# Modulation blocks 24 to 39 of a hybrid decoder layer, given other places in the order of the work

## The chip, the cores and the metric

The kernel runs on one core of a Trainium2 chip. The metric is the device time of one execution in microseconds (us). The kernel before was timed three times: 430.69, 431.64 and 430.80 us, median 430.8 us. The engines are TensorE (PE for the matmuls, PEld for their weight loads), VectorE (DVE), ScalarE (ACT), GpSimd (POOL) and SyncE (SP, which issues nearly all DMAs here).

## The reference

One layer of a decoder, 256 positions, width 1024, all in float32. A vector `c` conditions it, through a matrix of 6144 x 1024:

```python
mod = silu(c) @ w_ada + b_ada             # 6144 numbers: shift1 scale1 gate1 shift2 scale2 gate2
h = rms_norm(x, norm1_g) * (1 + scale1) + shift1
x = x + gate1 * mixer(h)                  # in-projection; attention and SSD; out-projection w_out
h = rms_norm(x, norm2_g) * (1 + scale2) + shift2
x = x + gate2 * conv_ffn(h)               # w_up, convolution over 3 positions, SwiGLU, w_down
```

The mixer projects `h` to q, k, v (8 heads of 128), z, x/B/C and dt. One half is causal softmax attention with normalized q and k. The other is a state-space part (SSD): convolution and SiLU on x/B/C, then for each of 16 heads a 256 x 256 causal matrix of decays times C·B, times x·dt, plus a skip term, times SiLU(z), normalized. Both halves, side by side, go through `w_out`.

## The kernel before, in words

Everything is transposed: channels on the 128 partitions, positions along the rows. Weights come as chunks of 128 x 1024 floats (512 KB), one DMA each on SP's queue (L146), into a ring of eight buffers `raw`. Nearly every chunk is split for a product of higher precision: ACT rounds it to `whi` (L189), DVE takes the rest into `wlo` (L191), and PE does three matmuls where one would stand (`mm3`, L344: whi·hhi, wlo·hhi, whi·hlo). A few chunks (`PLAIN`) go to PE unsplit, in plain float32 (L826).

The 6144 modulation numbers are 48 blocks of 128. A block is a tile `ada` of 128 x 1024 (512 KB, L152) from a ring of three buffers, and one DVE instruction multiplies it with silu(c) and sums along the row (`ada_dve`, L244 to L248). Blocks 0 to 15 (shift1, scale1) are needed at once and are done first. Blocks 16 to 23 are gate1, 24 to 31 scale2, 32 to 39 shift2; blocks 40 to 47 (gate2) go to POOL and ACT in the FFN. The eight gate1 values get their bias at unit 28 (L787); scale2 is used when the last stage before the FFN begins (L867), shift2 after that (L880).

The order is written as units of one weight chunk each. Unit 0 to 4 is the rest of z, 5 to 28 is q, k and v (four chunks for each half of q, of k and of v), 29 to 36 the part of the out-projection that reads the SSD, 37 to 44 the part that reads the attention. Side work is hung on units by the table `P` (L45): `put(u, f)` files a function under unit u and `side(u)` (L789) runs what is filed. `P['ada_u']` holds the 24 units at which blocks 16 to 39 are multiplied (L780 to L786). It is sorted before use (L118). The load of a block enters SP's queue behind the chunk that lies four units later (`ada_lead`, L119 to L125), or when the ring has a free buffer.

Outside the stretches marked by hand, PE, DVE, ACT and POOL are ordered by the framework's scheduler: it takes the program as recorded, plans times for it, and writes a fixed order for each engine. SP keeps the order in which the DMAs were recorded (L70). So another place for a block moves its own DMA and its own DVE instruction by hand, and what stands around them on every engine through the planner.

The steps that the prediction speaks of: `ab_load` (L573, one DMA of a row of sums, broadcast to 128 partitions, out of `acd`), `decay` (L580: ACT L584, L585 and L590, DVE L591), `ssd_y` (L595: PE L602 and L603, then DVE L604 and L606), `qk_evac` (L642: ACT L644 and L648), `qk_rsqrt` (L654), `k_scale` (L659: ACT L662), `qk_trans` (L664: PE L668), `scores` (L681: PE L683 and L684, DVE L689 to L692, ACT L694), `ptrans` (L707: PE L711), `pv` (L716: PE L719 and L720, DVE L724), `ssm_out` (L633, by `scaled` at L627: DVE L629, ACT L630, DVE L631), `attn_sum` (L727: PE L611).

Of the kernel before, what the change touches and what calls it, by code (L numbers as in the profile page):

```python
# [41 lines left out]
V_DTB = 326  # L42
V_ALL = 327

P = {'n2l': 6, 'sqa': 0, 'xr0': 0, 'scp': 1, 'vq': 1, 'v1': 6, 'n2': 4, 'hpx': [1, 0, 1, 0, 0, 1], 'e0': 0, 'ev': [1, 0, 1, 0], 'ada_u': [3, 4, 5, 5, 6, 7, 10, 9, 9, 19, 20, 20, 22, 24, 24, 25, 33, 35, 36, 37, 39, 39, 41, 42], 'ada_e': [1, 1, 1, 1, 1, 1, 1, 1, 1, 1, 1, 1, 1, 1, 1, 1, 1, 1, 1, 1, 1, 1, 1, 1], 'ada_lead': 4, 'ada_s': 0, 'g2': 68, 'hip': [0, 0, 0, 0, 0, 0, 0, 0, 0, 0, 0, 0, 0, 0, 0, 0, 0, 0, 0, 0, 0, 0, 0, 0, 0, 0, 0, 0, 0, 0, 1, 0, 0, 0, 1, 0, 0, 0, 0, 1, 0, 0, 0, 0, 0, 0, 0, 0, 0, 0, 0, 0, 0, 0, 0, 0, 0, 0, 0, 0], 'conv': [0, 0, 1, 0, 2, 5, 5, 4, 8, 4, 7, 6], 'dt': [1, 2, 2, 4], 'cdb': [7, 7], 'xbt': [9, 12, 11, 12], 'Y0': 14, 'DL': 3, 'ab0': 11, 'ss': 9, 'so': 2, 'qk': [12, 14, 17, 20, 21, 23], 'A0': 21, 'so1': 2, 'so2': 3, 'pv0': 26, 'sm_e': [0, 0, 1, 0, 1, 0, 0, 0], 'dc_e': [2, 2, 2, 0, 2, 2, 2, 0, 2, 2, 2, 0, 2, 2, 2, 0], 'mm_e': [1, 1, 1, 1, 1, 1, 1, 1, 1, 1, 1, 1, 1, 1, 1, 1], 'gz_e': [0, 0, 0, 0, 0, 0, 0, 0], 'sq_e': [1, 1, 1, 1, 1, 1, 1, 1], 'final': 2, 'ab_q': 0, 'LA': 2, 'asu': 34, 'aru': 38, 'aod': 2, 'w0': 4, 'w1': 4, 'w2': 4, 's1la': -1, 'zi': 1, 'lop': [0, 0, 0, 0, 0, 0, 0, 0, 0, 0, 0, 0, 0, 0, 0, 0, 0, 0, 0, 0, 0, 0, 0, 0, 0, 0, 0, 0, 0, 0, 0, 0, 0, 0, 0, 0, 0, 0, 0, 0, 0, 0, 0, 0, 0, 0, 0, 0, 0, 0, 0, 0, 0, 0, 0, 0, 0, 0, 0, 0], 'subs': [2, 1, 1, 1, 1, 1, 1, 1, 1, 1, 1, 1, 1, 1, 1, 1], 's1a': [0, 1, 0, 1, 0, 0, 0, 0]}  # L45

@with_exitstack
def mixer_ffn(ctx: ExitStack, tc: tile.TileContext, xT_d, c_d, vec_d, alog_d, ada_d,
# [24 lines left out]

    RAW, HL, ADA, LA = 8, 5, 3, P["LA"]
    raw_r = Ring(RAW, [128, 1024], "raw")
# [6 lines left out]
    for kt in range(KT):  # L82
        chunks.append((win1_d[kt, :, 0:1024], 1024))
        cuts.append(P["subs"][kt])
        if kt == 0:
            chunks.append((wv0_d, 1024))
            cuts.append(2)
        chunks.append((win1_d[kt, :, 1024:1936], 912))
        cuts.append(P["subs"][KT + kt])
    N1 = len(chunks)  # L90
# [11 lines left out]
    NCHUNK = len(chunks)  # L102
    items = [("a", 0), ("v", 0), ("a", 1)] if P["vq"] else [("a", 0), ("a", 1), ("v", 0)]
    for kt in range(KT):
        items.append(("w", 2 * kt + (kt > 0)))
        if kt == 0 and P["e0"] == 0:
            items.append(("w", 1))
        if kt < KT - 1:
            items.append(("a", 2 * kt + 2))
            if P["s1a"][kt]:  # L110
                items.append(("a", 2 * kt + 3))
# [953 lines left out]
```

## Time and profile before

| | |
|---|---|
| median of three runs | 430.8 us |
| profiled execution, its own time | 430.68 us |
| span of that execution | 429.0 us |
| PE busy, PEld busy | 422.5 us, 385.1 us |
| DVE busy, ACT busy, POOL busy | 344.4 us, 268.2 us, 26.0 us |
| DMA, mean over the span | 224 GB/s |

The span runs from the first to the last instruction of the profile; the time of the execution is 1.7 us longer. A busy share is an average over stages: up to about 60 us the first projection runs beside the first 16 modulation blocks, up to 84 us z, up to about 175 us q, k and v with the SSD and the first attention heads beside them, up to 233 us the out-projection, then the FFN. Instruction ends of PE are modelled and overlap the next start, so that a regular row of starts, and not the busy time, shows that PE is fed.

### The profile page before, as it was taken

To read this page: it belongs to the slowest core of one execution; us is meant where nothing else is said; L and a number is where in the kernel's file an instruction comes from. 1 tells how busy PE (TensorE), PEld (TensorE's weight loads), DVE (VectorE), ACT (ScalarE), POOL (GpSimd) and SP (SyncE) were. 2 spreads that over 40 slices of the span, in tenths; PEclk is the share of its full clock that TensorE was granted. 3 is DMA by queue.
4 is the path that set the end of the run, shared out by engine and by line. 5 is a ranking of instruction groups with operands and counts; after the bars stand their busy time and mean duration, and the time that the engine had idled before them with its cause. 6 is when DMAs were issued, how large, how long until landed. Compare 5 with 4: busy or idle time off the path is not lost.

```text
span 429.0 us, 7921 instructions
## 1 busy us (share of the span) xinstructions
PE 422.5 (98%) x3020; PEld 385.1 (90%) x3020; DVE 344.4 (80%) x680; ACT 268.2 (63%) x534; POOL 26.0 (6%) x24
## 2 busy tenths in 40 slices
PE   8999999999999999999999999999999999999996
PEld 8899998768767567889999999999999999999996
DVE  4779968999659888999999699778787877777755
ACT  4375448826999775886267495576666655555640
POOL 2000000000000001000000000222332200000000
PEclk9899999999999999999999999999999999999999
DMA  7999965889359549234691468767776665554002
GB/s 270 398 414 408 388 195 179 306 313 339 103 178 384 185 150 377 100 136 165 232 348 55 136 249 278 270 219 257 261 244 207 236 197 198 161 185 148 0 2 98
DMA packets 29589, 96.19 MB, mean 224 GB/s; under 512 B 3680, under 2 KB 6128, under 8 KB 29552
## 3 DMA queue, kind: packets, MB, share of 16 engines
q1 hardware_dynamic: 29520, 95.68, 62.5%
q8 instruction: 23, 0.38, 0.4%
q14 instruction: 14, 0.11, 0.1%
q10 hardware_dynamic: 32, 0.02, 0.0%
HBM read 94.62 MB, written 1.06 MB: 223 GB/s over the span
## 4 chain that ended last, share of the span: by engine, by line
PE 78%; DVE 9%; DMA 6%; ACT 5%; issue 1%; SPq 1%; ACTq 0%
PE bank L347 17%; PE bank L345 17%; PE bank L346 17%; PE bank L826 4%; PE bank L805 4%; PE bank L828 4%; DMA raw<-in_win_dram 4%; PE bank L829 4%; PE bank L830 4%; DVE wlo L191 2%; DMA vec<-in_vec_dram 2%; ACT whi L189 2%; DVE adax L246 2%; PE bank L931 2%; DVE ada L246 1%; PE bank L419 1%
## 5 line engine op out<-in xcount | busy, mean ns | idle before, releaser
L191 DVE TENSOR_TENSOR wlo<-raw,whi 128x1024 fp32r<-128x1024 f32 (+2 forms) x115 | 143.0, 1245 | 13.8 <-ACT whi L189 13.6
L189 ACT ACTIVATE whi<-raw 128x1024 fp32r<-128x1024 f32 (+2 forms) x112 | 115.0, 1035 | 40.8 <-PE bank L347 30.3
L347 PE MATMUL bank<-h2lo,whi 128*128 128x256 f32 x336 | 95.2, 283 | 0.0
L345 PE MATMUL bank<-h2hi,whi 128*128 128x256 f32 x336 | 95.2, 283 | 0.0
L346 PE MATMUL bank<-h2hi,wlo 128*128 128x256 f32 x336 | 95.1, 283 | 0.0
L916 DVE SCALAR_TENSOR_TENSOR fbuf<-bank,vec,fbuf 128x255 f32<-128x255 f32 (+1 forms) x84 | 40.2, 481 | 30.7 <-ACT fbuf L914 29.3
L347 PEld LDWEIGHTS bank<-h2lo,whi 128*128 128x128 f32 x336 | 64.5, 192 | 0.2 <-DVE h2lo L900 0.2
L345 PEld LDWEIGHTS bank<-h2hi,whi 128*128 128x128 f32 x336 | 64.5, 192 | 0.1
L346 PEld LDWEIGHTS bank<-h2hi,wlo 128*128 128x128 f32 x336 | 64.5, 192 | 0.0
L345 PE MATMUL bank<-fsp,whi 128*128 128x256 f32 x176 | 49.8, 283 | 0.0
L346 PE MATMUL bank<-fsp,wlo 128*128 128x256 f32 x176 | 49.8, 283 | 0.0
L347 PE MATMUL bank<-fsp,whi 128*128 128x256 f32 x176 | 49.8, 283 | 0.0
L914 ACT ACTIVATE fbuf<-bank,vec 128x256 f32<-128x256 f32 x42 | 23.4, 560 | 35.0 <-PE bank L347 35.0
L246 DVE SCALAR_TENSOR_TENSOR ada<-ada,cb 128x1024 f32<-128x1024 f32 x30 | 36.5, 1216 | 0.6 <-DMA ada<-in_ada_dram 0.6
L345 PEld LDWEIGHTS bank<-fsp,whi 128*128 128x128 f32 x176 | 33.8, 192 | 0.0
L346 PEld LDWEIGHTS bank<-fsp,wlo 128*128 128x128 f32 x176 | 33.8, 192 | 0.0
L347 PEld LDWEIGHTS bank<-fsp,whi 128*128 128x128 f32 x176 | 33.8, 192 | 0.0
L828 PE MATMUL bank<-whi,hhi 128*128 128x512 f32 x70 | 29.7, 429 | 0.0
L829 PE MATMUL bank<-wlo,hhi 128*128 128x512 f32 x70 | 28.9, 412 | 0.0
L830 PE MATMUL bank<-whi,hlo 128*128 128x512 f32 x70 | 28.3, 404 | 0.0
L251 POOL TENSOR_TENSOR ada<-ada,cb 128x1024 f32<-128x1024 f32 x8 | 19.8, 2474 | 114.9 <-DMA ada<-in_ada_dram 114.9
L419 PE MATMUL bank<-hhi,whi 128*128 128x256 f32 (+1 forms) x128 | 21.5, 292 | 0.0
(223 smaller groups left out, 830.9 us busy)
## 6 DMA issues: line engine op xcount, KB each, us to landing
raw<-in_wup_dram SPq DMA_DIRECT2D x44, 512.0 KB, 4.3
ada<-in_ada_dram SPq DMA_DIRECT2D x38, 512.0 KB, 5.3
raw<-in_wdn_dram SPq DMA_DIRECT2D x22, 512.0 KB, 3.7
raw<-in_winq_dram SPq DMA_DIRECT2D x16, 512.0 KB, 4.3
raw<-in_wout_dram SPq DMA_DIRECT2D x16, 512.0 KB, 4.7
adax<-in_ada_dram SPq DMA_DIRECT2D x10, 512.0 KB, 9.4
raw<-in_win_dram SPq DMA_DIRECT2D x8, 456.0 KB, 9.8
raw<-in_win_dram SPq DMA_DIRECT2D x7, 512.0 KB, 9.8
```

What stands on the lines that cost most here:

```text
L189: act.activation(hi[:, c], t[:, c], AF.Copy)
L191: (pool if lo_on_pool(i) else dve).tensor_tensor(lo[:, c], t[:, c], hi[:, c].bitcast(F32), op=OP.subtract)
L246: dve.scalar_tensor_tensor(t, t, 1.0, sc, op0=OP.mult, op1=OP.mult, accum_out=mod[:, i:i + 1])
L345: pe.matmul(out, w[0], h[0], start=start, stop=False, skip_group_check=True)
L346: pe.matmul(out, w[1], h[0], start=False, stop=False, skip_group_check=True)
L347: pe.matmul(out, w[0], h[1], start=False, stop=stop, skip_group_check=True)
L419: pe.matmul(s1_acc(i)[:m], w[k % 2], h[k // 2], start=(kt == k == 0 and i in (0, 2, 4, 6, 8, 10, 13, 14)), stop=last and kt == KT - 1, ski ...
L828: pe.matmul(bs[t], hhi[:, kt, blk(t)], w[0][:, wc], start=(q4 == k2 == 0), stop=False)
L829: pe.matmul(bs[t], hhi[:, kt, blk(t)], w[1][:, wc], start=False, stop=False)
L830: pe.matmul(bs[t], hlo[:, kt, blk(t)], w[0][:, wc], start=False, stop=(kt == KT - 1))
L914: act.activation(a, src, AF.Identity, bias=vec[:, V_FB + i:V_FB + i + 1], scale=vec[:, w + 2:w + 3])
L916: dve.scalar_tensor_tensor(a[:, s:], src[:, :S - s], vec[:, w + 2 - s:w + 3 - s], a[:, s:], op0=OP.mult, op1=OP.add)
```

## The change

One entry of the table `P` is other; the rest of the line, and of the kernel, is word for word the same. Of the 24 places, 20 stay; one at 24, and 35, 36 and one at 39 go, and 12, 13, 15 and 17 come. Blocks are handed to the sorted places in turn, so nearly every block from 23 on is multiplied earlier.

```diff
...
-'ada_u': [3, 4, 5, 5, 6, 7, 10, 9, 9, 19, 20, 20, 22, 24, 24, 25, 33, 35, 36, 37, 39, 39, 41, 42]
+'ada_u': [3, 4, 5, 5, 6, 7, 9, 9, 10, 12, 13, 15, 17, 19, 20, 20, 22, 24, 25, 33, 37, 39, 41, 42]
...
```

In units 29 to 44 there were eight places and there are five; one more leaves unit 24.

The first place is SP's queue, with the loads for the last chunks of k and the first of v. `raw` are weight chunks, `ada` modulation blocks; a `+` is a row of the changed kernel alone.

```order
 L146 DMA raw_73<-in_winq_dram 128x1024
 L146 DMA raw_74<-in_winq_dram 128x1024
+L152 DMA ada_91<-in_ada_dram 128x1024
 L146 DMA raw_75<-in_winq_dram 128x1024
+L152 DMA ada_92<-in_ada_dram 128x1024
 L146 DMA raw_76<-in_winq_dram 128x1024
 L146 DMA raw_77<-in_winq_dram 128x1024
+L152 DMA ada_93<-in_ada_dram 128x1024
 L146 DMA raw_78<-in_winq_dram 128x1024
 L146 DMA raw_79<-in_winv_dram 128x1024
```

Three block loads now stand between these chunks; the first rows of sums `ab` come right behind `raw_79` in both kernels, and have three more transfers ahead of them.

The second place is DVE between the scores of the third and fourth attention heads and the first normalized SSD rows (L629). First the kernel before:

```order
L691 TENSOR_REDUCE sm_802<-bank_65 128x1 x2
L191 TENSOR_TENSOR wlo_87<-raw_73,whi_82 128x1024
L692 TENSOR_TENSOR sm_802<-sm_802,rqk 128x2
L689 TENSOR_TENSOR bank_66<-bank_66,mask 128x2x128
L691 TENSOR_REDUCE sm_800<-bank_66 128x1 x2
L699 RECIPROCAL sm_802<-sm_802 128x2
L692 TENSOR_TENSOR sm_800<-sm_800,rqk 128x2
L705 TENSOR_SCALAR p_1465<-p_1465,sm_802 128x128
L705 TENSOR_SCALAR p_1465<-p_1465,sm_802 128x256
L309 COPY rssm<-bank_65 128x256
L640 TENSOR_TENSOR vS<-bank_69,vS 128x512
L629 SCALAR_TENSOR_TENSOR hbuf_166<-xsT,vec,rssm 128x256
```

Then the same place in the changed kernel:

```order
L691 TENSOR_REDUCE sm_802<-bank_65 128x1 x2
L309 COPY rssm<-bank_66 128x256
L692 TENSOR_TENSOR sm_802<-sm_802,rqk 128x2
L689 TENSOR_TENSOR bank_66<-bank_66,mask 128x2x128
L699 RECIPROCAL sm_802<-sm_802 128x2
L691 TENSOR_REDUCE sm_800<-bank_66 128x1
L309 COPY rssm<-bank_65 128x256
L691 TENSOR_REDUCE sm_800<-bank_66 128x1
L629 SCALAR_TENSOR_TENSOR hbuf_166<-xsT,vec,rssm 128x256
```

A split of a weight chunk (`wlo_87`), the two halves of L705 and the addition to v (L640) have gone from ahead of L629 to behind it.

The third place is PE in the first out-projection units: `bank_69` gathers the first, `bank_70` the third; L683 and L684 are the scores of the sixth head, and stand in the kernel before here:

```order
L347 MATMUL bank_70<-ylo,whi_82 128x256
L345 MATMUL bank_70<-yhi,whi_82 128x256
L346 MATMUL bank_70<-yhi,wlo_87 128x256
L347 MATMUL bank_69<-ylo,whi_85 128x256
L347 MATMUL bank_70<-ylo,whi_82 128x256
L683 MATMUL bank_65<-kT,qT 128x128
L684 MATMUL bank_65<-kT,qT 128x256
L711 MATMUL bank_67<-ident,p_1466 128x128
L345 MATMUL bank_69<-yhi,whi_85 128x256
L346 MATMUL bank_69<-yhi,wlo_90 128x256
```

In the changed kernel they stand here:

```order
L828 MATMUL bank_71<-whi_84,hhi 128x512
L829 MATMUL bank_71<-wlo_89,hhi 128x512
L830 MATMUL bank_71<-whi_84,hlo 128x512
L345 MATMUL bank_70<-yhi,whi_82 128x256
L683 MATMUL bank_65<-kT,qT 128x128
L684 MATMUL bank_65<-kT,qT 128x256
L711 MATMUL bank_67<-ident,p_1474 128x128
L345 MATMUL bank_69<-yhi,whi_85 128x256
L346 MATMUL bank_69<-yhi,wlo_90 128x256
```

The two scores stand 30 rows earlier, ahead of nearly all of the out-projection, and the first and third unit are no longer done in turns.

## Rows read from the trace of the kernel before

**Rows 1.** The line of the page that gives the span
```profile
span 429.0 us, 7921 instructions
```

**Rows 2.** Busy time by stretch: PE, PEld, DVE, ACT, POOL (count), granted clock, DMA share, GB/s
```profile
164.00:178.00 14.00, 13.56 (x78) 10.87 (x76) 12.39 (x41) 10.91 (x27) 0.48 (x1) 1.00 0.73 281
178.00:192.00 14.00, 13.08 (x98) 11.97 (x97) 13.49 (x40) 11.41 (x37) 1.05 (x1) 1.00 0.22 76
192.00:205.00 13.00, 12.82 (x101) 12.22 (x99) 12.71 (x23) 7.88 (x17) 1.58 (x1) 1.00 0.56 198
205.00:236.00 31.00, 30.80 (x249) 30.38 (x250) 30.06 (x63) 17.91 (x29) 0.00 (x0) 1.00 0.55 207
236.00:429.00 193.00, 189.51 (x1564) 188.50 (x1562) 143.28 (x223) 112.09 (x174) 19.80 (x8) 1.00 0.55 186
```

**Rows 3.** Waits of PE, 150 to 236 us: total, times, longest
```profile
PE bank L668 <- ACT qk L662: 0.4, 1, 0.4
PE bank L683 <- ACT p L694: 0.6, 1, 0.6
PE bank L719 <- DVE alo L724: 0.3, 1, 0.3
PE bank L611 <- DVE alo L724: 0.4, 1, 0.4
```

**Rows 4.** Timeline of PE around its two longest waits: start, length, work, idle before
```profile
163.92 0.39 PE L830 MATMUL bank<-whi,hlo 128*128 128x512 f32 x1
164.15 0.40 PE L828 MATMUL bank<-whi,hhi 128*128 128x512 f32 x1
164.99 0.62 PE L668 MATMUL bank<-ident,qk 128*128 128x128 f32 x2 [0.44 <-ACT qk L662]
179.17 0.28 PE L346 MATMUL bank<-yhi,wlo 128*128 128x256 f32 x1
179.29 0.40 PE L347 MATMUL bank<-ylo,whi 128*128 128x256 f32 x2
180.27 0.49 PE L683 MATMUL bank<-kT,qT 128*128 128x128 f32 x2 [0.58 <-ACT p L694]
```

**Rows 5.** Timeline of PE, first two pairs of state-space heads
```profile
114.76 0.66 PE L602 MATMUL bank<-m,xdt 128*64 128x256 f32 x4
120.08 0.66 PE L602 MATMUL bank<-m,xdt 128*64 128x256 f32 x4
```

**Rows 6.** Timeline of ACT, q's second half and the first decays
```profile
97.61 0.60 ACT L644 ACTIVATE qk<-bank 128x512 f32<-128x512 f32 x1 [0.73 <-PE bank L830]
109.19 0.51 ACT L584 ACTIVATE m<-ab,acum 128x256 f32<-128x256 f32 x1
114.36 0.57 ACT L672 ACTIVATE qT<-bank 128x512 f32<-128x512 f32 x1
118.13 0.50 ACT L584 ACTIVATE m<-ab,acum 128x256 f32<-128x256 f32 x1
```

**Rows 7.** Timeline of DVE, first product with a decay
```profile
112.26 0.56 DVE L591 TENSOR_TENSOR m<-m,cbm 128x384 f32<-128x384 f32 x1 [1.25 <-ACT m L590]
```

**Rows 8.** Issue of the first decay row by SP, and landing times of its tile
```profile
104.56 0.43 SPq L578 DMA_DIRECT2D ab<-acd  x1
DMA to landing us min/median/max: 2.8/4.2/8.7
```

**Rows 9.** Busy time by stretch, DMA share and GB/s in the last columns
```profile
96.00:100.00 4.00, 4.00 (x21) 3.26 (x20) 4.00 (x7) 3.24 (x13) 0.00 (x0) 1.00 1.01 399
100.00:104.00 4.00, 4.00 (x19) 3.26 (x18) 4.00 (x6) 3.39 (x12) 0.00 (x0) 1.00 0.96 351
```

**Rows 10.** Groups of DVE, 84 to 246 us: count, busy us, mean ns, idle before
```profile
L246 DVE SCALAR_TENSOR_TENSOR ada<-ada,cb 128x1024 f32<-128x1024 f32 x21 | 25.5, 1215 | 0.0
```

**Rows 11.** Timeline of ACT and DVE: second half of k, first state-space normalization
```profile
164.53 2.45 ACT L662 ACTIVATE qk<-qk,rqk 128x128 f32<-128x128 f32 x8 [1.96 <-DVE rqk L296]
174.36 1.27 DVE L629 SCALAR_TENSOR_TENSOR hbuf<-xsT,vec,rssm 128x256 f32<-128x256 f32 x3
```

More of the change, by code (lines that the diff above doesn't have):

```diff
@@ L43 @@
 V_ALL = 327
-P = {'n2l': 6, 'sqa': 0, 'xr0': 0, 'scp': 1, 'vq': 1, 'v1': 6, 'n2': 4, 'hpx': [1, 0, 1, 0, 0, 1], 'e0': 0, 'ev': [1, 0, 1, 0], 'ada_u': [3, 4, 5, 5, 6, 7, 10, 9, 9, 19, 20, 20, 22, 24, 24, 25, 33, 35, 36, 37, 39, 39, 41, 42], 'ada_e': [1, 1, 1, 1, 1, 1, 1, 1, 1, 1, 1, 1, 1, 1, 1, 1, 1, 1, 1, 1, 1, 1, 1, 1], 'ada_lead': 4, 'ada_s': 0, 'g2': 68, 'hip': [0, 0, 0, 0, 0, 0, 0, 0, 0, 0, 0, 0, 0, 0, 0, 0, 0, 0, 0, 0, 0, 0, 0, 0, 0, 0, 0, 0, 0, 0, 1, 0, 0, 0, 1, 0, 0, 0, 0, 1, 0, 0, 0, 0, 0, 0, 0, 0, 0, 0, 0, 0, 0, 0, 0, 0, 0, 0, 0, 0], 'conv': [0, 0, 1, 0, 2, 5, 5, 4, 8, 4, 7, 6], 'dt': [1, 2, 2, 4], 'cdb': [7, 7], 'xbt': [9, 12, 11, 12], 'Y0': 14, 'DL': 3, 'ab0': 11, 'ss': 9, 'so': 2, 'qk': [12, 14, 17, 20, 21, 23], 'A0': 21, 'so1': 2, 'so2': 3, 'pv0': 26, 'sm_e': [0, 0, 1, 0, 1, 0, 0, 0], 'dc_e': [2, 2, 2, 0, 2, 2, 2, 0, 2, 2, 2, 0, 2, 2, 2, 0], 'mm_e': [1, 1, 1, 1, 1, 1, 1, 1, 1, 1, 1, 1, 1, 1, 1, 1], 'gz_e': [0, 0, 0, 0, 0, 0, 0, 0], 'sq_e': [1, 1, 1, 1, 1, 1, 1, 1], 'final': 2, 'ab_q': 0, 'LA': 2, 'asu': 34, 'aru': 38, 'aod': 2, 'w0': 4, 'w1': 4, 'w2': 4, 's1la': -1, 'zi': 1, 'lop': [0, 0, 0, 0, 0, 0, 0, 0, 0, 0, 0, 0, 0, 0, 0, 0, 0, 0, 0, 0, 0, 0, 0, 0, 0, 0, 0, 0, 0, 0, 0, 0, 0, 0, 0, 0, 0, 0, 0, 0, 0, 0, 0, 0, 0, 0, 0, 0, 0, 0, 0, 0, 0, 0, 0, 0, 0, 0, 0, 0], 'subs': [2, 1, 1, 1, 1, 1, 1, 1, 1, 1, 1, 1, 1, 1, 1, 1], 's1a': [0, 1, 0, 1, 0, 0, 0, 0]}
@@ new lines @@
+P = {'n2l': 6, 'sqa': 0, 'xr0': 0, 'scp': 1, 'vq': 1, 'v1': 6, 'n2': 4, 'hpx': [1, 0, 1, 0, 0, 1], 'e0': 0, 'ev': [1, 0, 1, 0], 'ada_u': [3, 4, 5, 5, 6, 7, 9, 9, 10, 12, 13, 15, 17, 19, 20, 20, 22, 24, 25, 33, 37, 39, 41, 42], 'ada_e': [1, 1, 1, 1, 1, 1, 1, 1, 1, 1, 1, 1, 1, 1, 1, 1, 1, 1, 1, 1, 1, 1, 1, 1], 'ada_lead': 4, 'ada_s': 0, 'g2': 68, 'hip': [0, 0, 0, 0, 0, 0, 0, 0, 0, 0, 0, 0, 0, 0, 0, 0, 0, 0, 0, 0, 0, 0, 0, 0, 0, 0, 0, 0, 0, 0, 1, 0, 0, 0, 1, 0, 0, 0, 0, 1, 0, 0, 0, 0, 0, 0, 0, 0, 0, 0, 0, 0, 0, 0, 0, 0, 0, 0, 0, 0], 'conv': [0, 0, 1, 0, 2, 5, 5, 4, 8, 4, 7, 6], 'dt': [1, 2, 2, 4], 'cdb': [7, 7], 'xbt': [9, 12, 11, 12], 'Y0': 14, 'DL': 3, 'ab0': 11, 'ss': 9, 'so': 2, 'qk': [12, 14, 17, 20, 21, 23], 'A0': 21, 'so1': 2, 'so2': 3, 'pv0': 26, 'sm_e': [0, 0, 1, 0, 1, 0, 0, 0], 'dc_e': [2, 2, 2, 0, 2, 2, 2, 0, 2, 2, 2, 0, 2, 2, 2, 0], 'mm_e': [1, 1, 1, 1, 1, 1, 1, 1, 1, 1, 1, 1, 1, 1, 1, 1], 'gz_e': [0, 0, 0, 0, 0, 0, 0, 0], 'sq_e': [1, 1, 1, 1, 1, 1, 1, 1], 'final': 2, 'ab_q': 0, 'LA': 2, 'asu': 34, 'aru': 38, 'aod': 2, 'w0': 4, 'w1': 4, 'w2': 4, 's1la': -1, 'zi': 1, 'lop': [0, 0, 0, 0, 0, 0, 0, 0, 0, 0, 0, 0, 0, 0, 0, 0, 0, 0, 0, 0, 0, 0, 0, 0, 0, 0, 0, 0, 0, 0, 0, 0, 0, 0, 0, 0, 0, 0, 0, 0, 0, 0, 0, 0, 0, 0, 0, 0, 0, 0, 0, 0, 0, 0, 0, 0, 0, 0, 0, 0], 'subs': [2, 1, 1, 1, 1, 1, 1, 1, 1, 1, 1, 1, 1, 1, 1, 1], 's1a': [0, 1, 0, 1, 0, 0, 0, 0]}
```

## The prediction

> **What bounds the kernel.** I read the span first [rows 1], then the busy times by stretch [rows 2], then PE's waits [rows 3] and the timeline around them [rows 4], and only then the engines that PE waits for. The reader should see that PE bounds nearly everything. From 236 us to the end, in the FFN, the two kernels are the same, so that stretch adds nothing to either side. From 205 to 236 us DVE is busy 30.06 of 31 us, and yet PE is busy 30.80 [rows 2]: the splits are made well ahead, and a full DVE costs PE almost nothing there. This matters, because it is mainly there that the change relieves DVE. What PE does lose lies between 164 and 192 us: 0.44 us in the first of the two stretches and 0.92 us in the second [rows 2].
>
> The waits name the places [rows 3]: 0.4 us for k that ACT has yet to scale, 0.6 us for a softmax that frees a bank, 0.3 us for DVE's L724, and at about 205 us another 0.4 us for the last L724. The starts give a little more. From 163.92 to 164.15 us is one regular step, 0.23 us; the next is 0.84, so 0.61 are lost. From 179.17 to 179.29 is a regular step of 0.12; the next two matmuls take 0.98 us, so 0.74 are lost [rows 4]. With the 0.3 for L724 that is 1.65 us before 192 us, against 1.3 us by the waits alone. I call 1.5 us the sum that can be won there.
>
> A rule of the Trainium skill would have more to win. From 164 to 178 us PEld is busy 10.87 of 14 us, from 178 to 192 us 11.97 of 14 [rows 2]. "Perfetto Trace Analysis", section "Identifying the Most-Contended Engine", says that the busy share of matmuls tells little of the distance to the roofline, and that the share of weight loads should be read for it. By that PE would have 3.1 + 2.0 = 5.1 us of headroom in these 28 us, where the regular starts leave 1.5. The starts of the 512-column matmuls follow each other at 0.23 us with a short weight load under each, so I go by the starts.
>
> **The change, part by part.** *PE* keeps every instruction, and the cost of that is zero. *DVE* keeps its 24 products of 1.2 us (21 of them after 84 us, 25.5 us together [rows 10]). Three of eight leave the units of the out-projection. By the order, the two that stand ahead of the attention's sum (L611) have successors in the same places; those that go are later, where PE waits for nothing. I take 0 for their leaving, at best the 0.20 us that PE misses from 205 to 236 us [rows 2].
>
> *SP.* Three loads, 1.57 MB, are put ahead of the first rows `ab`. In those us the DMA engines are full, at 399 and 351 GB/s [rows 9], so the rows land 3.9 to 4.5 us later. Before, the first was issued at 104.56 us [rows 8], and ACT began with it at 109.19 us without a wait [rows 6], so it had landed; now it should have landed by 113.7 us. The planner has moved ACT's first decay too: behind the evacuation of q's second half (two L644, one L672, five L648, one split). Before, one L672, two L644 and eight L648 took from 114.36 to 118.13, 3.8 us [rows 6]; three L648 less and one split of about 1 us more leave that the same. The evacuation can start when PE has done units 9 to 12: 48 matmuls of 0.23 us from 97.6 us on [rows 4, 6], with 2 us allowed for transposes between them, an estimate of 110.6 us. So the first decay comes at about 114.5 instead of 109.2, and its product on DVE at 112.26 + 5.3 = 117.6 us [rows 7]. PE in turn reads it later: eight transposes and a plain chunk, which stood between the first and the second pair of heads, now stand ahead of both. From the first pair to the second it is 5.3 us; some 0.8 of it is the pair itself (0.66 us for its L602), the rest, 4.5 us, now comes first: 114.76 + 4.5 = 119.3 us [rows 5]. There are 1.6 us in hand. Beside it, three products on DVE, 3.6 us, fall into a stretch where it waited anyway (1.25 us before one L591 alone [rows 7]). Cost: 0 if the cover holds, and if the rows come late up to 2 us, worked out below. I take 0.1, because the later pairs have less in hand than the first.
>
> A rule that speaks against the change: in this trace the products on DVE wait for nothing, 0.0 us before 21 of them [rows 10]. "TensorE: Matmul & The Clock Gate", section "Architectural detail: the array is 16× 32×32, not 1× 128×128", says that ACT and DVE take their queues strictly in order, so that a product whose block has not landed holds up every split and decay behind it. With full DMA engines the new products could be the first to do this. By the worst landing of `ab` against the median, 8.7 and 4.2 us [rows 8], such a hold is 4.5 us at most; 1.25 of these DVE idles anyway before L591 [rows 7] and 1.6 are in hand, so the sum would rise by 1.7 us. It would add to the late case below, and the 0.0 us say that it has not happened here so far.
>
> *From 134 to 192 us* both orders hold five products until the last half of v, so the new products are past when k is normalized. Two things then come earlier on DVE. The chain of the reciprocal root for the first half of k has one split between its short steps instead of three, by the order, which is an estimated 2 us; the second half follows. And ahead of L629 a split of 1.2 us and an addition to v are gone. So the scores and L629, before at 174.36 us [rows 11], should come 2 to 4 us earlier. The wait at 164.99 ended with L662 at 164.53, which had itself waited 1.96 us for the root [rows 11]. But the planner has also moved what PE does: the sixth head's scores stand 30 rows earlier, 30 x 0.12 = 3.6 us, and k's transposes about half a unit. Supply comes 2 to 4 us earlier, demand about 2 to 3.6. If the lead is at its upper end, the 1.5 us are won; at its lower end nothing is, or PE waits a little longer. I take two thirds, 1.0 us, since the first three of the four places depend on the lead of the chain, and the split that has gone from it is certain by the order. The 0.4 us at 205 us stays: the last pv and L611 are moved about as far as the work ahead of them.
>
> **Sum.** 430.68 us is the profiled execution's own time. 430.68 - 1.0 + 0.1 - 0.0 = 429.8 us. The median of the runs shown is 0.1 us above that execution, which I leave inside the rounding. Predicted: 429.8 us.
>
> **Rivals.**
> *The lead is handed on (no change).* The scheduler plans every reader to come just when its data does, so that a DVE that is 2 to 4 us ahead meets a PE order that asks as much sooner, and the same 1.5 us are lost in other places. For it: the two shifts are equal within what I can work out. Against: the interleaving of two out-projection units is gone, as if the planner saw nothing to wait for. Time: 430.68 - 0.2 = 430.5 us.
>
> *The decays come late (slower).* The place is PE's first four pairs of L602. If the `ab` rows take their worst landing, 8.7 us, and 4.5 us more, they land at 117.8 instead of 113.3 us, 3.3 us after ACT's turn at 114.5; 1.6 are in hand, 1.7 are paid by PE, and 0.5 more at the next pairs. It decides from the moment the first row lands after about 116.1 us. Nothing is won later, since the SSD's normalization then starts late too. Time: 430.68 + 2.2 = 432.9 us at worst, 431.9 us in the middle. For it: DMA engines full at 351 to 399 GB/s just there [rows 9]. Against: the median landing is 4.2 us, and ACT did not wait.
>
> *PE has more headroom than its starts show (much faster).* That is the weight-load rule as a mechanism: a third of 5.1 us more than I count would come back where DVE is relieved, 430.68 - 1.0 - 1.7 = 428.0 us. The regular starts speak against it.
>
> **How the numbers follow.** Forecast, 428.9 to 430.1 us: 0.42. Lead handed on, 430.1 to 431.2: 0.31. Decays late, 431.2 to 432.9: 0.24. More headroom, 428.0: 0.03. 0.2% of the median, 0.86 us, is about what a measurement of this kernel can tell from no change; it lies at 429.94 and 431.66. A little of the forecast's weight lies above 429.94, and a part of the late case below 431.66: faster 0.42, same 0.34, slower 0.24. The range that leaves out no more than 2 in 10 is 428.8 to 432.0; the forecast's own is 428.9 to 430.1.
>
> **What would show it.** Right, if PE's first L602 starts near 119 us with no wait before it and ACT's first L584 near 114.5; if L629 starts at 170 to 172 us; if the waits at L668 and L683 fall under 0.3 us each; and if DVE has idle time between 205 and 236 us while PE's busy time there does not change. Wrong, if PE waits for L591 or ACT for `ab` between 112 and 125 us, if L246 waits for its DMA, or if the losses before L683, L719 and L611 are the same 1.5 to 2 us in other places.

## The result, and the profile after

The changed kernel took 435.73 us (median of 4 runs, 435.12 to 436.51), the kernel before 430.91 beside it (430.69 to 431.64). The ratio is 1.0104 with a 95% interval of 1.0091 to 1.0117: 4.5 us slower by the ratio, far outside the 429.8 us forecast and above the 432.0 at which the range ended.

The page of the changed kernel gives a span that is 5.8 us longer than before [rows 1]:

```profile
span 434.8 us, 7920 instructions
```

Of these 5.8 us, 0.8 lie ahead of everything that changed: the first matmul of the projections behind z (L826) starts at 83.45 us in the profile of before and at 84.25 in this one, and at 83.4 to 85.2 us in the other kernels. So I compare the *stretch* from there to the start of the last L347, which leaves both ends out: 341.80 us before, 346.84 after, **+5.04 us**. One profile gives each stretch; for all kernels but one (`products_planned`, below) it differs from before's by what the medians differ by, to within some 0.7 us.

The windows of the kernel after, with the columns of [rows 2] (busy us of PE, PEld, DVE, ACT, POOL with counts, granted clock, DMA share, GB/s), and two short ones, the first as an answer to [rows 9], the last at the largest loss:

```profile
108.00:112.00 4.00, 4.00 (x28) 3.42 (x27) 3.74 (x6) 1.81 (x3) 0.00 (x0) 1.00 1.02 416
...
178.00:192.00 14.00, 11.48 (x69) 9.83 (x68) 12.26 (x36) 11.12 (x33) 1.06 (x1) 0.88 0.11 38
...
205.00:236.00 31.00, 30.89 (x260) 30.69 (x259) 27.62 (x56) 16.12 (x27) 1.05 (x1) 1.00 0.51 176
...
181.10:185.50 4.40, 4.35 (x18) 3.46 (x18) 3.89 (x13) 3.61 (x13) 0.00 (x0) 0.61 0.00 0
```

The hole is from 178 to 192 us: 69 matmuls where there were 98, and a mean granted clock of 0.88. DVE has 2.4 us less to do from 205 to 236, and PE is as busy there as it was: a relief of the wrong engine at a place where it bounded nothing.

PE's waits from 96 to 236 us (reader, what it waited for, total, times, longest), beside [rows 3] for the part from 150 us on:

```profile
PE bank L683 <- ACT p L694: 2.0, 1, 2.0
PE bank L829 <- DVE wlo L191: 1.1, 1, 1.1
PE bank L719 <- DVE alo L724: 0.5, 1, 0.5
PE bank L300 <- DVE rt L296: 0.4, 1, 0.4
PE bank L602 <- DVE m L591: 0.2, 1, 0.2
```

The wait at L668 is gone, as forecast, and that at L611, which I had expected to stay; but L683 went from 0.6 to 2.0, and one at L829 is new. All waits come to 4.2 us against 1.7 in [rows 3], which explains 2.5 of the 5 us. The rest is not waiting but time that PE is "busy": it shows in the timeline, in which three places matter most.

**Pairs of heads set apart.** PE's timeline (start, length, engine, line, work, in brackets the idle time ahead and what ended it):

```profile
125.46 0.65 PE L602 MATMUL bank<-m,xdt 128*64 128x256 f32 x2 [0.23 <-DVE m L591]
...
126.26 0.50 PE L828 MATMUL bank<-whi,hhi 128*128 128x512 f32 x1
126.69 0.65 PE L602 MATMUL bank<-m,xdt 128*64 128x256 f32 x2
...
127.48 0.50 PE L829 MATMUL bank<-wlo,hhi 128*128 128x512 f32 x1
130.24 0.66 PE L602 MATMUL bank<-m,xdt 128*64 128x256 f32 x4
...
131.04 0.50 PE L828 MATMUL bank<-whi,hhi 128*128 128x512 f32 x1
...
140.41 0.50 PE L829 MATMUL bank<-wlo,hhi 128*128 128x512 f32 x1 [1.06 <-DVE wlo L191]
...
178.81 0.28 PE L345 MATMUL bank<-yhi,whi 128*128 128x256 f32 x1
181.11 0.49 PE L683 MATMUL bank<-kT,qT 128*128 128x128 f32 x2 [2.01 <-ACT p L694]
...
191.54 0.70 PE L719 MATMUL bank<-pT,vS 128*128 128x256 f32 x2 [0.47 <-DVE alo L724]
```

A pair of state-space heads works in two halves of the array's columns (`128*64`). The pair at 130.24 takes 0.80 us to the next matmul (130.24 to 131.04). The pair at 125.46 has been pulled apart by a plain matmul: its first head takes 0.80 us (125.46 to 126.26), its second 0.79 (126.69 to 127.48). Half the work costs all the time. The Trainium skill, "TensorEngine Tiling (Array Packing)", section "Key Properties", says that tiles of the array work independently and side by side; this trace agrees, 0.80 us for two heads together and for one alone. The first pair, too, is in pieces after: its heads come one behind the other, and from its first matmul at 119.86 us to the next other one it takes 1.31 us. So is the eighth: a transpose (L668) stands behind its first matmuls, which take 0.58 us to it (from 148.14 us), and the rest takes 0.80 (from 148.98). Added up in this way, the eight pairs take 8.3 us after and 7.3 before. Before has one pair apart too, the seventh, which is together after. PE's timeline of the kernel before at that place:

```profile
140.97 0.65 PE L602 MATMUL bank<-m,xdt 128*64 128x256 f32 x2
142.82 0.65 PE L602 MATMUL bank<-m,xdt 128*64 128x256 f32 x2
```

**A split behind a blocked instruction.** At 140.41 PE waits 1.06 us for a weight split, at 181.11 for a bank. DVE's timeline at the first of these and at the first L629:

```profile
138.74 0.48 DVE L604 SCALAR_TENSOR_TENSOR xsT<-xsT,vec,bank 128x256 f32<-128x256 f32 x1 [0.70 <-PE bank L603]
139.14 1.22 DVE L191 TENSOR_TENSOR wlo<-raw,whi 128x1024 fp32r<-128x1024 f32 x1
...
173.54 0.87 DVE L629 SCALAR_TENSOR_TENSOR hbuf<-xsT,vec,rssm 128x256 f32<-128x256 f32 x2
```

The split that PE wants at 139.35 is queued behind an L604 that itself waits 0.70 us for PE's heads. Had it stood ahead, from 138.04 us on, it would have been done at 139.3.

**The scores ahead of the out-projection.** ACT's timeline, whose first row answers to the first decay in [rows 6]:

```profile
115.59 0.51 ACT L584 ACTIVATE m<-ab,acum 128x256 f32<-128x256 f32 x1
...
179.02 1.05 ACT L189 ACTIVATE whi<-raw 128x1024 fp32r<-128x1024 f32 x1
179.98 0.44 ACT L694 ACTIVATE p<-bank,sm,rqk 128x128 f32<-128x128 f32 x1
180.41 0.55 ACT L694 ACTIVATE p<-bank,sm,rqk 128x256 f32<-128x256 f32 x1
```

L683 needs the bank that L694 empties, and a 1.05 us split stands ahead of L694. PE has nothing else to do in its order, since the rows that stood ahead of L683 before are now behind it, and waits 2.01 us. In the stretch behind it (181.1 to 185.5 us) the granted clock is 0.61, a part of it thus at 1.2 instead of 2.4 GHz. From L683 to the L719 at 191.54 us it takes 10.43 us, which an experiment below compares with the same rows at full clock. DVE's L640, which stood ahead of L629 before, now comes at 181.81 us.

### The profile page after: what moved, and what is told of

Read it like the earlier page. It is cut to its first block, busy times and chain, and to the rows that moved or that the text cites. A ratio compares the mean times of both kernels' runs of the same rounds, so it can differ in the third digit from the quotient of the medians.

```text
span 434.8 us, 7920 instructions
## 1 busy us (share of the span) xinstructions
PE 425.2 (98%) x3020; PEld 386.9 (89%) x3020; DVE 347.5 (80%) x680; ACT 268.2 (62%) x534; POOL 24.8 (6%) x24
## 3 DMA queue, kind: packets, MB, share of 16 engines
HBM read 94.62 MB, written 1.06 MB: 220 GB/s over the span
## 4 chain that ended last, share of the span: by engine, by line
PE 75%; DVE 11%; DMA 7%; ACT 4%; issue 1%; SPq 1%; ACTq 0%
PE bank L347 17%; PE bank L345 17%; PE bank L346 17%; PE bank L805 4%; DMA raw<-in_win_dram 4%; PE bank L826 4%; DVE wlo L191 3%; PE bank L829 3%; PE bank L830 3%; PE bank L828 3%; DMA adax<-in_ada_dram 2%; DVE adax L246 2%; PE bank L931 2%; PE bank L419 1%; DVE ada L246 1%; ACT whi L189 1%
## 5 line engine op out<-in xcount | busy, mean ns | idle before, releaser
L347 PE MATMUL bank<-h2lo,whi 128*128 128x256 f32 x336 | 95.3, 284 | 0.0
L345 PE MATMUL bank<-h2hi,whi 128*128 128x256 f32 x336 | 95.3, 284 | 0.0
L347 PEld LDWEIGHTS bank<-h2lo,whi 128*128 128x128 f32 x336 | 63.4, 189 | 0.2 <-DVE h2lo L900 0.2
L345 PEld LDWEIGHTS bank<-h2hi,whi 128*128 128x128 f32 x336 | 63.4, 189 | 0.1
L346 PEld LDWEIGHTS bank<-h2hi,wlo 128*128 128x128 f32 x336 | 63.4, 189 | 0.0
L347 PE MATMUL bank<-fsp,whi 128*128 128x256 f32 x176 | 49.8, 283 | 0.0
L345 PE MATMUL bank<-fsp,whi 128*128 128x256 f32 x176 | 49.8, 283 | 0.0
L246 DVE SCALAR_TENSOR_TENSOR ada<-ada,cb 128x1024 f32<-128x1024 f32 x30 | 36.5, 1216 | 0.6 <-DMA ada<-in_ada_dram 0.6
L347 PEld LDWEIGHTS bank<-fsp,whi 128*128 128x128 f32 x176 | 33.2, 189 | 0.0
L345 PEld LDWEIGHTS bank<-fsp,whi 128*128 128x128 f32 x176 | 33.2, 189 | 0.0
L829 PE MATMUL bank<-wlo,hhi 128*128 128x512 f32 x70 | 28.3, 404 | 1.1 <-DVE wlo L191 1.1
```

The costliest lines, as they stand in the source:

```text
L246: dve.scalar_tensor_tensor(t, t, 1.0, sc, op0=OP.mult, op1=OP.mult, accum_out=mod[:, i:i + 1])
L345: pe.matmul(out, w[0], h[0], start=start, stop=False, skip_group_check=True)
L346: pe.matmul(out, w[1], h[0], start=False, stop=False, skip_group_check=True)
L347: pe.matmul(out, w[0], h[1], start=False, stop=stop, skip_group_check=True)
L829: pe.matmul(bs[t], hhi[:, kt, blk(t)], w[1][:, wc], start=False, stop=False)
```

## The experiments

Two means recur. *Held to an order*: from about 95 to 245 us every instruction of PE, ACT and DVE, the modulation products excepted unless the text says otherwise, is tied to the one that stood ahead of it in a given order, so that the planner can rearrange nothing there:

```diff
+    for eng, seq in ORD.items():          # ranks of the other kernel
+        mine = [i for i in nc.cur_bb.bb.instructions if ... and i.name not in st["prod"]]
+        for x, y in zip(seq, seq[1:]):
+            tc.add_manual_dep(mine[y], mine[x].name, ...NoSync...)
```

And *pairs together*: the first head of a pair may start only when the decays of the second are there:

```diff
-        (dve if P['mm_e'][h] else pool).tensor_tensor(m, m, cbm[:, h // 8], op=OP.mult)
+        X["mi", h] = (dve if P['mm_e'][h] else pool).tensor_tensor(m, m, cbm[:, h // 8], op=OP.mult)
...
-            pe.matmul(o[:, 0:256], xdt[:, 0, hs], m[:, 0:256], start=True, ...)
+            i0 = pe.matmul(o[:, 0:256], xdt[:, 0, hs], m[:, 0:256], start=True, ...)
+            j or tc.add_manual_dep(i0.ins, X["mi", h + 1].ins.name, ...Sync...)
```

**1. The moves or the orders?** The loads and products of the change with the orders of before, the reverse, and the change with the orders of before in its late part only.

> The changed kernel's loads and products, in its own places, but PE, ACT and DVE (without the modulation products) held to the order of the kernel before from about 95 to 245 us. Theory A (the new order loses the time: heads of a pair apart, no other work beside the late scores): with the order of before the loss is gone, 430 to 431.5 us. Theory B (the three loads put ahead of the rows `ab` make them land some 5 us later, and the new order only follows that): ACT stands at its first decay at about 110 us until the rows land at about 114 to 115, PE waits 3 to 5 us at its first pair of L602, 434 to 436 us.

> The loads and products of the kernel before, in their places, but PE, ACT and DVE (without the modulation products) held to the order of the changed kernel from about 95 to 245 us. Theory A (order): the loss is there without the early loads and products, 434 to 436 us. Theory B (loads): rows `ab` and decays are ready early, little is lost, 431 to 432.5 us, the rest being heads of pairs apart.

> The changed kernel, with PE, ACT and DVE held to the order of before only from about 155 us (DVE), 168 us (PE) and 171 us (ACT) on: the addition to v (L640) and the split wlo_87 stand ahead of L629 again and PE has out-projection rows ahead of the seventh scores. Theory A: the 2.0 us wait at L683 and the granted clock of 0.79 behind it are gone, 2.0 to 2.5 us come back, 433.2 to 433.8 us. Rival: PE is so late there that the same time is lost at another place, 435 to 436 us.

Measured: `orders_before` 434.67 us, ratio 1.0073 [1.0052, 1.0093], stretch +3.06; `orders_after` 438.67 us, 1.0170 [1.0149, 1.0191], +7.53; `late_orders_before` 434.44 us, 1.0072 [1.0057, 1.0087], +3.08. So the moves alone cost 3.1 us even where nothing else moves, and the orders of after cost more with the old loads and products than with the new: this order goes with these moves. The late part of the new orders costs 1.96 us (5.04 - 3.08). The waits of `orders_before` say where 2.4 of the 3.06 are:

```profile
PE bank L568 <- DVE xdt L569: 1.4, 1, 1.4
PE bank L602 <- DVE m L591: 1.0, 2, 0.7
```

Two products (1.2 us each) stand ahead of L569 on DVE, and the decays come late, so that the first pair's two heads are done one after the other.

**2. The pairs.** After and before, each with the pairs together.

> The changed kernel with one more dependence: the first L602 of a pair of heads waits for the decay product of the second head too. Only two pairs on PE move, a few rows later; nothing else moves on any engine. Theory A (two heads done apart cost 0.8 us more than side by side, since their 64-column tiles no longer run together): 1.3 to 1.7 us come back by 127 us; if they last, 434.0 to 434.4 us. Rival (PE meets the split wlo that it waits for at 140 us just the same, so that what comes back is waited away there): 435.2 to 435.8 us.

> The kernel before with the one dependence of the run with pairs together: the first L602 of a pair of heads waits for the second head's product. Its seventh pair, which it does in two halves at 141.0 and 142.8 us, comes together. If two halves cost 0.8 us more than a pair, and nothing else is late: 430.5 to 430.9 us, faster than both. Rival (the chunk in plain float32 that stood between the halves, or a later wait, takes it): 431.2 to 431.7 us.

Measured: `pairs_together` 434.38 us, 1.0070 [1.0046, 1.0094], stretch +3.57, so 1.47 us back. And **430.10 us** for before with the same edit, 0.9972 [0.9962, 0.9982] over 8 runs against 24 of before (431.35): a version that beats both kernels. Before has its seventh pair apart, at 140.97 and 142.82 us (shown above). With the edit it is one, again 0.80 us to the next matmul, in PE's timeline of `pairs_before`:

```profile
142.77 0.66 PE L602 MATMUL bank<-m,xdt 128*64 128x256 f32 x4
...
143.57 1.13 PE L826 MATMUL bank<-raw,h 128*128 128x512 f32 x2
```

**3. Loads or products?** The kernel before with four loads more at the change's places (into a tile that is free then), or four products more, filed there (on data that lie in SBUF), each held to the order of before and then with the planner free.

```diff
-        items.append(("w", i))
+        items.extend([("w", i)] + [("a", 100 + k) for k, u in enumerate((12, 13, 15, 17)) if i == N1 + u + P["ada_lead"]])
...
+    [put(u, lambda k=k: dve.scalar_tensor_tensor(kT..., sc, 1.0, sc, ...)) for k, u in enumerate((12, 13, 15, 17))]; ...
```

> The kernel before, its order held on PE, ACT and DVE, with four more loads of 512 KB behind the chunks where the changed kernel has them (into the tile of k, which is idle then); no product is moved or added. Theory L (the loads make the rows `ab` late): ACT's first decay waits, PE waits at its first pairs of L602, 432.5 to 434 us. Theory P (the products ahead of other work on DVE cost the time): 431.0 to 431.6 us, as before.

> The kernel before, its order held, with four more products of 1.2 us on DVE at the four places where the run with the orders of before has its early ones, on data that is there; no load is added or moved, and the late products stay. Theory P: PE waits 1.4 us at L568 for L569, which stands behind two products, and about 1 us at L602 for L591, 433 to 434.5 us. Theory L: DVE has room there, 431.0 to 431.8 us.

> The kernel before with the four more loads of the run with the loads alone, but with no order held: the planner may answer them. By the order it puts the first decays behind the evacuation of q, as in the changed kernel, and sets the heads of the first and the third pair apart. If its answer is no better than the late rows themselves (two pairs apart, 0.8 us each, in place of 2 us of waits): 432.6 to 433.6 us. Rival (its answer hides the late rows, as the forecast had it): 431.3 to 432.0 us.

> The kernel before with four more products on DVE at 12, 13, 15 and 17 and no more loads, with no order held; the planner puts one of them into the first stage, since it waits for nothing. If the planner plans well around products alone: 431.2 to 432.0 us. Rival (any change of its input costs this order a us or more): 432.5 to 434 us.

| run | median us | ratio [95%] | stretch |
|---|---|---|---|
| loads, held | 433.19 | 1.0040 [1.0024, 1.0057] | +2.06 |
| products, held | 432.05 | 1.0016 [1.0007, 1.0025] | +1.08 |
| loads, planner free | 433.86 | 1.0059 [1.0042, 1.0075] | +2.81 |
| products, planner free | 432.45 | 1.0029 [1.0018, 1.0040] | +0.02 |

In the held kernels the two add up to the 3.06 of `orders_before` within 0.1 us, and each shows one of its waits. The loads, in the waits of ACT, DVE and PE from 96 to 142 us:

```profile
ACT m L584 <- DMA ab<-acd: 3.6, 1, 3.6
DVE m L588 <- DMA ab<-acd: 6.0, 3, 3.1
PE bank L602 <- DVE m L591: 1.7, 2, 1.5
```

ACT and DVE wait for the rows `ab` (in before DVE 1.6 us and ACT not at all), and PE pays 1.7 us. The products:

```profile
PE bank L568 <- DVE xdt L569: 1.3, 1, 1.3
```

With the planner free, the loads alone cost no less: 0.75 us more by the stretch, while the intervals of the two ratios overlap. It lets ACT and DVE come to the rows later, so that they wait 0.3 and 0.8 us for them, but it sets the first and third pairs apart, as after has them in pieces, and puts the same split behind the same L604:

```profile
PE bank L829 <- DVE wlo L191: 1.1, 1, 1.1
PE bank L683 <- ACT p L694: 0.6, 1, 0.6
```

But its L683 is the 0.6 of before: the late rearrangement does not come from the loads alone. To the products the planner has another answer, and it makes this run no test of them: since they wait for nothing, it puts all four into an earlier stage, 40 us ahead of their places and ahead of the stretch. From the view of their line in `products_planned`:

```profile
L787 DVE SCALAR_TENSOR_TENSOR kT<-cb x4: 1218/1221/1227, 60.3 to 65.3; 128x1024 f32<-128x1024 f32 x4
```

There PE waits 1.1 us for DVE, and the first L826 comes at 85.18 us. So the median is 1.1 us longer though the stretch isn't, and what the planner would do with products at the change's places this run does not show. This is the one kernel in which the two measures part.

**4. The late part: wait, clock or bank?** The changed kernel held to its own orders, with 16 and then 9 matmuls on constants in the wait, to keep PE busy; then with L640 eight places earlier and 12 rows of the out-projection ahead of the scores.

```diff
+    FILL = [pe.matmul(bank[7][:, 0:128], ident, ident, start=True, stop=True, ...).ins for _ in range(9)]
...
+            run = [mine[seq[383]]] + FILL + [mine[seq[384]]]
```

> The changed kernel, its order held, with sixteen matmuls of 128x128 on constants into an idle bank behind the first L345, where PE waits 2.0 us for L683; their result is not used. They take some 1.8 us of that wait. If the granted clock of 0.61 in the 4.4 us behind the wait comes of PE's idling, it stays at 1.00 and 1.4 to 1.7 us come back: 434.0 to 434.4 us. Rival (the clock falls for another reason, or the scores then wait for DVE just as long): 435.4 to 436 us.

> As the run with the stall filled, but with nine matmuls, 0.22 us each by that run, so 2.0 us, the length of the wait, and with the modulation products held too, one of which had slipped ahead there. If the granted clock of 0.61 behind the wait comes of PE's idling, it stays at 1.00 and 1.4 to 1.7 us come back: 434.0 to 434.4 us. Rival (what the clock gives back is waited away for DVE and ACT within the next heads): 435.2 to 435.8 us.

> The changed kernel, its whole order held, the products too, with two moves: on DVE the addition to v that frees the bank of the first out-projection unit (L640, at 181.8 us) 8 places earlier, where its input is ready, and on PE that unit's first twelve matmuls (1.4 us) ahead of the seventh scores. If PE idles there because its own other work was put behind, and its bank was not freed: the wait at L683 falls under 1 us, the clock stays at 1.00, 1.5 to 2.5 us come back: 433.2 to 434.2 us. Rival (the scores, now later, make the later heads late by as much): 435.2 to 435.8 us.

Measured: `stall_filled` 437.03 us, 1.0132 [1.0118, 1.0146]; `stall_filled_9` 435.62 us, 1.0100 [1.0085, 1.0115]; `rows_first` 435.37 us, 1.0091 [1.0074, 1.0108]. The first is inconclusive: 16 fills took 3.6 us (0.22 each), longer than the wait, and a product slipped ahead on DVE. The other two end the low clock. The window of `stall_filled_9`, whose order is after's but for the fill, and its PE timeline:

```profile
181.00:185.50 4.50, 4.10 (x28) 3.60 (x28) 4.38 (x15) 4.50 (x16) 0.00 (x0) 1.00 0.00 0
...
178.73 0.28 PE L345 MATMUL bank<-yhi,whi 128*128 128x256 f32 x1
...
181.03 0.49 PE L683 MATMUL bank<-kT,qT 128*128 128x128 f32 x2
...
190.33 0.70 PE L719 MATMUL bank<-pT,vS 128*128 128x256 f32 x2 [0.47 <-DVE alo L724]
...
217.31 0.43 PE L300 MATMUL bank<-ident,rt 128*128 128x128 f32 x2 [0.75 <-DVE rt L296]
```

and those of `rows_first`:

```profile
181.00:185.50 4.50, 3.59 (x22) 2.56 (x20) 4.00 (x15) 4.50 (x17) 0.00 (x0) 1.00 0.00 0
...
179.35 0.28 PE L345 MATMUL bank<-yhi,whi 128*128 128x256 f32 x1
...
190.85 0.70 PE L719 MATMUL bank<-pT,vS 128*128 128x256 f32 x2 [0.44 <-DVE alo L724]
```

L683 comes 2.30 us behind the first L345 in `stall_filled_9` as in after. From it to the L719 that waits for L724 it is 9.30 us (181.03 to 190.33) instead of 10.43 (181.11 to 191.54), with the same rows in the same order: 1.13 us is what the low clock costs there. A part of it is lost again later, where PE waits 0.75 us at an L300 at which it does not wait in after. In `rows_first`, from the first L345 to that L719 it is 11.50 us instead of 12.73, and to the last L347 1.43 us less than in after (250.85 instead of 252.28), 0.71 less in `stall_filled_9`.

Over the whole run less of this is left. The stretches are 4.05 (`rows_first`) and 4.81 (`stall_filled_9`) above before's, where after's is 5.04; the medians are 0.4 and 0.1 us under after's, and the intervals of the ratios overlap with after's. Some 0.45 us were lost ahead of the place: PE waited 0.6 and 0.7 us for an L591 at the third pair, after 0.2. Whether this comes of holding the products or of chance, no run shows. `rows_first` has new waits in its late part:

```profile
PE bank L711 <- ACT pT L713: 0.7, 1, 0.7
PE bank L711 <- ACT p L703: 0.6, 1, 0.6
```

So the low clock makes up about 1.1 us of the late part at its place, and PE's own rows in the wait, with the clock that they keep up, give back 1.43 of the 1.96. The rest stays: behind the scores stands the softmax chain on ACT and DVE, and a PE that comes to it sooner waits there.

**5. The relief, and other places.** Four products of the out-projection left out, first with the products free, then with everything held; and the four put behind the rows of sums, at units 18 and 21.

> The kernel before, its order held, with the four products and loads at 24, 35, 36 and 39 left out: blocks 36 to 39 are not computed. This is what the out-projection can gain at most by being relieved. The forecast's own step says up to 1.0 us: 430.0 to 430.6 us. Rival (DVE there is ahead of PE anyway): 431.0 to 431.5 us, no change.

> The kernel before, with the products and loads of blocks 30, 33, 34 and 36 left out (those at the second 24, 35, 36 and the first 39; their numbers are zero), and every other instruction of PE, DVE, ACT held in the order of before, the products too. It is the most that the relief can give in that order. The forecast took 1.0 us from it: 430.4 to 430.8 us. Rival (in a fixed order PE waits there for ACT and for its own earlier work, not for these products): 431.2 to 431.7 us.

> The kernel before, its order held, with the same four products gone from 24, 35, 36 and 39, and put at 18, 18, 21 and 21, so that their loads stand behind the rows `ab` and no product is added on DVE before about 130 us. If the loss comes from the stretch of 100 to 122 us (loads ahead of the rows, products ahead of L569 and L591): 430.3 to 431.5 us, no loss. Rival (three products more ahead of L629 hold up the scores and the first out-projection units wherever they stand): 432.5 to 434.5 us.

Measured: `late_left_out` 441.21 us, 1.0216 [1.0200, 1.0232]; `late_left_out_held` 431.12 us, 0.9991 [0.9982, 1.0000]; `behind_rows` 437.18 us, 1.0129 [1.0114, 1.0144]. Leaving work out made the first 9.7 us slower. DVE's waits tell why, and PE's what it did to PE:

```profile
DVE ada L246 <- DMA ada<-in_ada_dram: 8.8, 1, 8.8
PE bank L300 <- DVE rt L296: 8.5, 1, 8.5
```

One product was queued ahead of its block's landing and held DVE for 8.8 us, with the root that PE needs behind it. Held, the relief is worth 0.4 us (0.0 to 0.8): the wait at L611 goes, and those at L668, L683 and L719 stay at 0.4, 0.6 and 0.3. (The forecast took 0 to 0.2 us from the products' leaving; its 1.0 us was for a lead on DVE.) Put behind the rows, the loads make chunks of v's weights late. PE waits for k's scaling, and ACT comes to that only behind a split that waited for its chunk, in PE's waits and ACT's timeline:

```profile
PE bank L668 <- ACT qk L662: 3.6, 1, 3.6
...
152.19 1.06 ACT L189 ACTIVATE whi<-raw 128x1024 fp32r<-128x1024 f32 x1 [2.67 <-DMA raw<-in_winv_dram]
153.15 2.43 ACT L662 ACTIVATE qk<-qk,rqk 128x128 f32<-128x128 f32 x8
```

The root that L662 needs was done by 148.3 us there, so it is the chunk and not the products on DVE that L662 waited for last.

**6. All three repaired.** The change with its pairs together, the split ahead of L604, and the late orders of before.

> The changed kernel with three repairs of its order, held: the two pairs of heads together (as in the run with pairs together), the split wlo that PE waits for at 140 us ahead of the L604 it stood behind on DVE, and from about 155 to 171 us on the order of before (as in the run with the late orders of before). If the three losses are separate, their sum comes back, 1.5 + 1.1 + 2.0 = 4.6 us: 431.1 to 432.0 us, within 0.5 us of before. Rival (PE, once earlier, meets the next late producer): half of it, 432.8 to 434 us.

Measured: 431.86 us, 1.0010 [1.0000, 1.0019], stretch +0.98. Its waits from 150 us on:

```profile
PE bank L683 <- ACT p L694: 0.6, 1, 0.6
...
PE bank L611 <- DVE alo L724: 0.4, 1, 0.4
```

With 0.4 at L300 and 0.3 at L719 these are nearly before's [rows 3]. By the ratios the three repairs give back 1.0104 - 1.0010, or 4.1 of 4.5 us, and by the stretch 4.06 of 5.04. The late order gave 1.96 of these and the pairs 1.47 in runs of their own; the 0.63 left for the split is a difference (346.84 - 1.47 - 1.96 - 342.78) and no price of it, since PE's wait for the split was 1.06 and is gone. The pairs are not repaired here as in `pairs_together`: they stand together in the order, but nothing makes the first head wait for the second one's decay, and PE, now earlier, does two of them one head after the other. The third, in PE's timeline:

```profile
125.64 0.90 PE L602 MATMUL bank<-m,xdt 128*64 128x256 f32 x3
...
126.91 0.50 PE L829 MATMUL bank<-wlo,hhi 128*128 128x512 f32 x1
```

It takes 1.27 us, and the fifth 1.28 (from 132.76 us), 0.95 more than two pairs of 0.80. So the 0.98 us that are left are not shown to be a price of the moves. Against before, all eight pairs lose 0.73 us here: these two and the eighth (0.57), less the 0.79 that before loses at its seventh.

After's own trace adds up in much the same way: 2.5 us more of waits, 1.05 more for the pairs (8.31 instead of 7.26) and 1.13 for the low clock make 4.7 of the 5.04.

## Why the prediction was wrong

Its views were read rightly and its nearest steps held. Its signs and sum did not.

- **"PE keeps every instruction, and the cost of that is zero": this step failed first.** The instructions are the same, but two heads in one place take 0.80 us and in two places 1.59. After has the first and third pairs in pieces, and the eighth; `pairs_together` gave back 1.47 us. The order that I had before me shows a plain matmul between the two heads of the third pair, where before there is none. I looked for where PE's rows went, not for what stood side by side.
- **"From 134 to 192 us: -1.0" was +1.96.** The step said that the scores and L629 would come 2 to 4 us earlier and that 1.5 us could be won. L629 came at 173.54, or 172.7 with the later start taken off, so 1.6 us earlier [rows 11], not 2 to 4; the wait at L668 went, and that at L683 grew to 2.0. The step counted what was gone from ahead of L629 (a split, an addition to v) as a gain, and did not ask who waits for these, nor what ACT had ahead of L694. It had the 30 rows that stood no longer ahead of the scores, 3.6 us of demand brought forward, and set them against a lead that was not there. In `rows_first` 1.43 of it came back in the late part; the low clock, a cost that the step did not have, is 1.13 us at its place.
- **"SP: +0.1" was 2.8 with the planner's answer to the loads, 2.1 without.** ACT's first L584 came at 115.59 (114.8 with the start taken off, 114.5 forecast) and without a wait, PE's first L602 at 119.86 (119.1; 119.3 forecast). The rows landed no later than feared: 5.4 us in the median, 9.3 at worst, against 4.2 and 8.7 [rows 8], with the DMA engines full at 416 GB/s behind the stretch of [rows 9]. DVE waited 1.6 us for them, as in before. What failed is the price put on the cover: it was not slack that hid the late rows but a new order around them, and that costs by itself, in pairs apart (part of the 1.47 above) and a split that comes late (1.06 us of waiting).
- **"Three products fall into a stretch where it waited anyway": 1.1 us in the old order.** DVE's idle 1.25 us ahead of L591 [rows 7] was no cover there, since L569 stands between the products and PE, and PE waited 1.3 us at L568. In the changed kernel PE does not wait at L568; what the new order around the products costs, no run shows by itself.
- **"I take 0 for their leaving" held** within the noise (0.4 us [0.0 to 0.8] in `late_left_out_held`), and so did "a full DVE costs PE almost nothing" from 205 to 236 us: DVE 27.62 us instead of 30.06, PE 30.89 instead of 30.80 [rows 2]. From 236 us on the two are the same within 0.4 us.
- **The rivals.** *Decays late* was what the loads do in the old order: in `loads_alone` ACT waits 3.6 us for `ab` and PE 1.7 for the decays; at 433.19 us it is 1.7 us above the 431.52 of before beside it, where the rival said 1.2 to 2.2. In the changed kernel the planner has moved ACT's turn behind the rows, so the rival is not what made it slow. *The lead is handed on* is what the late part tends to in `rows_first`, where PE's waits move to L711. *More headroom* found nothing in any run; the weight-load rule is not borne out here. The hold of a product on its block, from the Trainium skill, "TensorE: Matmul & The Clock Gate", section "Architectural detail: the array is 16× 32×32, not 1× 128×128", which I weighed at 4.5 us at most, did not occur in the changed kernel (0.0 us before 22 of its L246), but the trace of `late_left_out` agrees with it, and at 8.8 us.

What stays open: the 0.5 us of the 1.96 that did not come back in `rows_first`, and how the wait and the late L640, both changed there, share the rest beside the clock; what the split costs by itself; and what brought the planner to the late rearrangement. The loads alone do not cause it, the products alone were not tried at their places with the planner free, and a run with only the late products gone and the planner free was not made.

## What to carry to other kernels

A change of a few places in a table is a change of the whole order: hold the old order and move only the loads or only the products, and you see what the move costs and what the planner made of it. Look in the trace whether an added instruction ran where it was put: four products that waited for nothing ran 40 us early. Count in the new order not only the instructions but which of them still stand side by side, and for each one that is now later, who waits for it. When an order shows such a thing, look for it in the kernel before too: the pair found apart there was worth 0.28%.

## What the runs showed of the hardware

- Two heads of 64 columns cost 0.80 us together and 0.80 each apart; one pair joined in the kernel before gave 0.8 us of stretch and 1.25 us of median.
- After 2.0 us without a matmul PE's granted clock was 0.61 on average in the next 4.4 us, so that part of them ran at 1.2 instead of 2.4 GHz; with the gap filled it was 1.00. The same rows from L683 to L719 took 10.43 us with the drop and 9.30 without; over the whole run the filled kernel was only 0.1 us faster by the medians, 0.2 by the stretch.
- Matmuls of 128x128 on constants took 0.22 us each in a row, 16 of them 3.6 us.
- One DVE instruction waiting 8.8 us for a transfer cost PE 8.5 us (`late_left_out`).
